# A third group of units in seven forms in one of three gate and up stages of a two-layer trunk

## The chip, the cores and the metric

The kernel runs on one core of a Trainium2 chip. The metric is the device time of one launch in microseconds. The kernel before takes 996.65 us, the median of three runs (996.29 to 997.11).

## The reference, cut to what matters

The trunk has two layers over 256 tokens of width 1024. Each layer is a feed-forward block, a token mixer and a second feed-forward block:

```python
def swiglu(h, w_gate_up, w_down):
    a, b = jnp.split(h @ w_gate_up, 2, axis=-1)
    return (jax.nn.silu(a) * b) @ w_down
...
    x = x + 0.5 * swiglu(rms_norm(x, ffn1_norm), ffn1_w_gate_up, ffn1_w_down)
    h = rms_norm(x, mix_norm)
...
    x = x + merged @ w_out
    x = x + 0.5 * swiglu(rms_norm(x, ffn2_norm), ffn2_w_gate_up, ffn2_w_down)
```

`w_gate_up` is 1024 x 5632 and `w_down` 2816 x 1024, all in float32. The mixer (causal pooling and attention in 256-position blocks, merged by gates) is not touched.

## The kernel before, in words

**Units.** All weights come from DRAM in units of 128 x 2048 float32 (1 MB). A gate and up stage has 22 of them (NF), each with 128 columns of the gate and 128 of the up projection; a down stage has 11. A unit lands in a tile `raw` (four buffers) and is split into `hi` and `lo`, two half tiles each (six half tiles of each kind, so three units): ScalarE copies to float32r (`hi`), VectorE subtracts (`lo`). x is held split in the same way (`hx`). A product of two split operands is then hi by hi and hi by lo' in one 512-wide matmul, and lo by hi in a 256-wide one; a whole unit is 32 matmuls (`pair`), drained from PSUM by one copy and one addition (`drain`).

**Seven forms.** In three of the four gate and up stages, groups of four units are computed in a Strassen scheme. The group's 2 x 2 blocks of weights are combined into seven forms "1" to "7", each of 1 MB and each worth 16 matmuls, so seven half units of work in place of eight. Forms 1, 2 and 3 are blocks of the weights as they are; forms 7, 6, 5 and 4 are sums that POOL's DMAs have written to DRAM before (tiles `f4` to `f7`; `far_sums` lists eight steps for each group, and each call of `go_on` sends one, behind the last marked VectorE instruction). The other operand is a form of x as well: `x_forms` makes four of them (7, 6, 5, 3) on ScalarE and VectorE after unit 2 (XF); forms 1, 2 and 4 use `hx` itself. A group's results have tokens on the partitions and are turned by eight transposes on TensorE (`turned`) before the down stage uses them. Several forms add up in one PSUM bank: 1, 6, 5, 3 in one, 7 and 4 in another, 2 in a third, and between two of them ScalarE or VectorE reads the sum.

**Order.** `feed_order` is a table written out by hand: numbers are whole units, "1A" is form 1 of group A. It is at once the order of the loads on SP's queue, of the splits and of the products on TensorE, which keeps program order. `post` (three VectorE operations, a Silu and a copy) finishes each pair of whole units. Group A is units 12 to 15, group B units 18 to 21.

In the stage that the change is about, the second layer's first gate and up stage (508 to 622 us in the profile), the order before is: 0, 1, 1A, 2, 2A, 3, 4, 7A, 5, 6A, 6, 5A, 7, 4A, 3A, 8, transposes, 1B, 9 with transposes in its middle, 2B, 10, 7B, 11, 6B, 16, 5B, 17, 4B, 3B, and then the down units.

Lines in the profile of before: L99 all matmuls, L549 the transposes, L176 and L177 the two splits of a form (ScalarE, VectorE), L187 and L188 those of a unit, L236 and L237 the drain, L443 to L452 `post`, L497 to L514 `x_forms`, L540 and L541 the gating of a group's results, L566 to L579 what else is done to its banks, L161 POOL's steps.

Of the kernel before, what the change touches and what calls it, by code (L numbers as in the profile page):

```python
# [25 lines left out]
P = 128  # L26
# [17 lines left out]

FU = NF + NF // 2 + 24
LU = FU + NF + NF // 2
GROUPS = {"A": 12, "B": 18}
XF = 2
SHIFT = 16
RAW = {"1": "11", "2": "21", "3": "22"}  # L50
SUMS = (("7", "12", "22"), ("6", "7", "11"), ("5", "11", "12"), ("4", "6", "21"))


def feed_order():

    return [0, 1, "1A", 2, "2A", 3, 4, "7A", 5, "6A", 6, "5A", 7, "4A", "3A", 8, "1B", 9, "2B", 10, "7B", 11, "6B", 16,
            "5B", 17, "4B", "3B"]


def feed_units(base):  # L60
    return [base + n if isinstance(n, int) else (base, n) for n in feed_order()]


C_G1, C_GM, C_G2, C_BG, C_PS, NG = 0, 8, 16, 24, 40, 44
# [3 lines left out]
def trunk_kernel(ctx: ExitStack, tc: tile.TileContext, x_in, w_in, pw_in, qkn_in, rope_in, mask_in, band_in, out):  # L68
# [78 lines left out]
        return z.rearrange("p (i c) -> p i c", i=2)  # L147

    def far_sums(base):
        steps_left.extend((base, g, f, src, kw) for g in GROUPS for f, one, two in SUMS  # L150
                          for src, kw in ((one, {}), (two, {"accum_op": OP.add})))

    def go_on():
# [241 lines left out]
    def bc2(a):  # L395
        return a.unsqueeze(1).to_broadcast([P, 2, a.shape[-1]])

    def ffn(after, n0=0, end=False, col=None, base=0, far_at=()):
        gs, gt = {}, {}

        def room(name, n0, m):
            g = acts.tile([P, m, 2, S], F32R, name=name, tag=name)
            gt[name] = g
            gs.update({n0 + i: g[:, i] for i in range(m)})
# [7 lines left out]
        room("gc", 8, 4)  # L412
        room("gd", 12, 4)
        abs_, more = {}, []
        late_r = not end
        last = {}

        def wide(n):
# [36 lines left out]
        if n0:  # L455
# [6 lines left out]
            for i in range(n0 + 1, NF + 1):  # L462
                if i < NF:
                    pair(unit(), wide(i))
                    fetch()
                    if i >= 8 and i % 3 == 2:
                        go_on()
                if i == NF or i % 3 != 1:
                    for n in range(done, NF if i == NF else min(done + 2, i - 1), 2):
                        scaled = post(n)  # L470
                        done = n + 2
                        if i == n0 + 1:
                            behind(scaled, drained[-1])
        else:
# [6 lines left out]
            columns(ws[1], pss[1], range(4, NK))  # L481
            drain(wide(1), pss[1])

            pre = acts.tile([P, 12 * S], F32, name="pre", tag="gb")
            vt = acts.tile([P, 2, GW], F32, name="vt", tag="v")
            tk = {g: acts.tile([P, 2, GW], F32, name="tk", tag="tok", bufs=2) for g in GROUPS}
            xg = pre[:, :NK * S].rearrange("p (k s) -> p k s", s=S)
            gq = {tn: vt[:, tn // 2, tn % 2 * S:(tn % 2 + 1) * S] for tn in range(4)}
            sf = {}
# [3 lines left out]
            def x_forms():  # L493

                late = drained[-1]
                for k in range(NK):
                    behind(act(xg[:, k, :], x[:, k, :], AF.Copy, scale=gain[:, l_of[0], col + k:col + k + 1]), late)  # L497
                (a11, a21), (a12, a22) = ([z[:, :, t * P:(t + 1) * P] for t in range(2)] for z in (xg[:, :4], xg[:, 4:]))
                s1, s2 = (pre[:, (8 + 2 * i) * S:(10 + 2 * i) * S].rearrange("p (k s) -> p k s", s=P) for i in range(2))
                s3, s4 = (vt[:, i, :].rearrange("p (k s) -> p k s", s=P) for i in range(2))  # L500
                fs = iter(eight(F32R, "sf", SHIFT))

                def parts_of(n, z):
                    sh, sl = (next(fs).rearrange("p (k s) -> p k s", s=P) for _ in range(2))
                    act(sh, z, AF.Copy)
                    tt(sl, z, sh.bitcast(F32), op=OP.subtract)
                    sf[n] = [(sh[:, k, :], sl[:, k, :]) for k in range(4)]

                tt(s3, a11, a21, op=OP.subtract)
                tt(s1, a22, a21, op=OP.subtract)  # L510
                parts_of("7", s3)
                stt(s2, s1, -1.0, a11, op0=OP.mult, op1=OP.subtract)
                parts_of("5", s1)
                stt(s4, s2, -1.0, a12, op0=OP.mult, op1=OP.subtract)  # L514
                parts_of("6", s2)
                parts_of("3", s4)
                room("gb", 16, NF - 16)

            def by_tokens(f, ps, first):

# [22 lines left out]

            def turned(n, g):

                pt = quarter("pt")
                for i in range(2):
                    for t in range(2):
                        keep(nc.tensor.transpose(pt[:, i, t * P:(t + 1) * P], gq[2 * t + n][:, i * P:(i + 1) * P], ident))  # L549
# [5 lines left out]
            bank = {}  # L555

            def strassen(f, g):

                b = ("x" if f in "1653" else "z" if f == "2" else "y") + g
                if b not in bank:  # L560
                    bank[b] = quarter("p" + b).rearrange("p a s -> p (a s)")
                z = bank[b]
                by_tokens(f, z, f in "127")
                p1, w = tk[g][:, 0], tk[g][:, 1]
                if f == "1":
                    act(p1, z, AF.Copy)  # L566
                elif f == "2":
                    tt(p1, z, p1, op=OP.add)
                    gated(p1, 0, 0, 0)
                elif f == "6":  # L570
                    act(w, z, AF.Copy)
                elif f == "5":
                    act(p1, z, AF.Copy)
                    tt(p1, bank["y" + g], p1, op=OP.add)
# [7 lines left out]
            due = None  # L582
            wait = [0, 1]
            for n in feed_order()[2:]:
                if isinstance(n, str):
                    strassen(*n)
                    if n[0] == "3":
                        due = n[1]
                    continue
                if due == "A0":  # L590
                    pair(unit(), wide(n), lambda: turned(0, "A"), NK // 2)
                    due = None
                else:
                    pair(unit(), wide(n))
                fetch()
                if due == "A":
                    turned(1, due)
                    due = "A0"
                if n in (6, 11):
                    go_on()  # L600
                if n == XF:
                    x_forms()
                if n % 2 and n > 1:
                    post(wait[0])
                    wait = [n - 1, n]
            post(wait[0])
            if due:
                last = {(1, 0): lambda: turned(1, due), (1, 5): lambda: turned(0, due)}
# [23 lines left out]
    def add_x(f, ps, two, r):  # L632
        t = x[:, f, :]
        if two:
            t = small.tile([P, S], F32, name="t", tag="sg", bufs=2)
            act(t, ps[:, 1, :], AF.Copy)
            if r is not None:
                tt(t, ps[:, 0, :], t, op=OP.add)
                stt(t, t, 0.5, r, op0=OP.mult, op1=OP.mult)
                marks.append(tt(x[:, f, :], x[:, f, :], t, op=OP.add))  # L640
                return
            stt(t, t, 0.5, x[:, f, :], op0=OP.mult, op1=OP.add)
        stt(x[:, f, :], ps[:, 0, :], 0.5, t, op0=OP.mult, op1=OP.add)

    def tokens():
# [107 lines left out]
    def mix(l, after):  # L753
# [150 lines left out]
        for h in range(NH):  # L904
            gate(h, *((lambda: score_two(h // 2), NK // 2) if h % 4 == 0 else ()))
            if h == 4:
                for p, y in enumerate(ys):
                    heads_end(p, y)
                known = soften_two()
            elif h < 2:  # L910
                soften(h)
            elif h % 4 == 2:
                turn_two(h // 4 * 2, (0, 1) if h > 4 else ())
            elif h == 3:
                pool_diff()
            open_gate(h)
            if h >= 3:
                go_on()

        def branch(f, j, k0=0, k1=4):  # L920
# [87 lines left out]
    for l in range(L):  # L1008
        l_of[0] = l
        if l == 0:  # L1010
            for base in STAGES:
                far_sums(base)
        ffn(lambda f: prep(f, l, C_GM), len(w3) if l == 0 else 0, col=C_G1, base=l * LU, far_at=(1, 3, 5, 7, 9))
        if l == 0:
            for d, z in ((rope, rope_in), (mask, mask_in), (qkn, qkn_in)):
                nc.sync.dma_start(d, z)
        mix(l, lambda f: prep(f, l, C_G2))
        if l + 1 < L:
            ffn(lambda f: prep(f, l + 1, C_G1), col=C_G2, base=FU, far_at=(1, 3, 5, 7, 9))
# [92 lines left out]
```

## Time and profile before

| | |
|---|---|
| profiled execution, own time | 996.52 us |
| its span, first to last instruction | 994.7 us |
| granted TensorE clock | 1.000 |
| busy share of the span: PE, VectorE (DVE), ScalarE (ACT), POOL | 99%, 81%, 65%, 6% |
| the stage from 508 to 622 us: PE, DVE, ACT busy | 114.0, 101.4, 86.8 us |
| DMA in that stage | 273 GB/s, 0.81 of 16 engines busy |

The profile comes from one execution, so a sum over its rows is to be set against 996.52 us. PE is TensorE's matmuls and PEld its weight loads; both overlap. In the rows of the chain of work the columns are start, duration, engine, tile, line and count. In rows of a timeline they are start, duration, engine, line, operation, out<-in, shapes and count, with the idle time before and what ended it in brackets.

### The profile page before, as it was taken

To read this page: it belongs to the slowest core of one execution; us is meant where nothing else is said; L and a number is where in the kernel's file an instruction comes from. 1 tells how busy PE (TensorE), PEld (TensorE's weight loads), DVE (VectorE), ACT (ScalarE), POOL (GpSimd) and SP (SyncE) were. 2 spreads that over 40 slices of the span, in tenths; PEclk is the share of its full clock that TensorE was granted. 3 is DMA by queue.
4 is the path that set the end of the run, shared out by engine and by line. 5 is a ranking of instruction groups with operands and counts; after the bars stand their busy time and mean duration, and the time that the engine had idled before them with its cause. 6 is when DMAs were issued, how large, how long until landed. Compare 5 with 4: busy or idle time off the path is not lost.

```text
span 994.7 us, 16119 instructions
## 1 busy us (share of the span) xinstructions
PE 989.5 (99%) x6312; PEld 898.6 (90%) x6312; DVE 801.1 (81%) x1136; ACT 651.4 (65%) x974; POOL 55.8 (6%) x95
## 2 busy tenths in 40 slices
PE   9999999999999999999999999999999999999998
PEld 8998888898899988889988889888989998888897
DVE  6987777698978799886779888676988888988862
ACT  7865555567756787675578677555677568776641
POOL 0000001002100100000000000000021000000000
PEclk9999999999999999999999999999999999999999
DMA  8878899964889999798966979897858895787740
GB/s 298 319 259 284 249 306 294 293 195 182 275 249 308 351 286 335 251 336 261 300 240 244 299 270 308 304 282 265 261 184 251 268 296 207 260 291 254 254 148 22
DMA packets 45243, 262.11 MB, mean 263 GB/s; under 512 B 4400, under 2 KB 5680, under 8 KB 22448
## 3 DMA queue, kind: packets, MB, share of 16 engines
q1 hardware_dynamic: 34992, 210.76, 57.9%
q0 software_dynamic: 10176, 50.33, 21.2%
q8 instruction: 49, 0.80, 0.3%
q14 instruction: 26, 0.21, 0.1%
HBM read 260.03 MB, written 51.38 MB: 313 GB/s over the span
## 4 chain that ended last, share of the span: by engine, by line
PE 99%; DMA 0%; ACT 0%; DVE 0%; SPq 0%; issue 0%
PE ps L99 72%; PE pt L99 7%; PE two L99 4%; PE pxB L99 3%; PE pxA L99 3%; PE pyA L99 2%; PE pyB L99 2%; PE pe L99 1%; PE sc L99 1%; PE pzB L99 1%; PE pzA L99 1%; PE pt L549 1%; PE pt L739 1%; PE y L99 1%; DMA raw<-w 0%; PE tp L695 0%
## 5 line engine op out<-in xcount | busy, mean ns | idle before, releaser
L188 DVE TENSOR_TENSOR lo<-raw,hi 128x1024 fp32r<-128x1024 f32 (+2 forms) x319 | 378.2, 1197 | 112.5 <-ACT hi L187 110.8
L187 ACT ACTIVATE hi<-raw 128x1024 fp32r<-128x1024 f32 (+2 forms) x319 | 327.8, 1036 | 198.6 <-PE ps L99 126.0
L99 PE MATMUL ps<-hx,hi 128*128 128x512 f32 x1312 | 443.2, 384 | 0.6 <-ACT hi L187 0.6
L99 PE MATMUL ps<-hx,lo 128*128 128x256 f32 x1312 | 358.7, 273 | 0.0
L99 PEld LDWEIGHTS ps<-hx,hi 128*128 128x128 f32 x1312 | 246.2, 188 | 44.6 <-ACT hi L187 0.8
L99 PEld LDWEIGHTS ps<-hx,lo 128*128 128x128 f32 x1312 | 246.5, 188 | 0.3 <-DVE lo L188 0.3
L177 DVE TENSOR_TENSOR lo<-raw,hi 128x1024 fp32r<-128x1024 f32 x84 | 102.2, 1221 | 23.8 <-ACT hi L176 23.7
L176 ACT ACTIVATE hi<-raw 128x1024 fp32r<-128x1024 f32 x84 | 88.9, 1059 | 46.8 <-PE ps L99 31.5
L99 PE MATMUL ps<-ga,hi 128*128 128x512 f32 (+1 forms) x264 | 87.9, 378 | 0.0
L99 PE MATMUL ps<-ga,lo 128*128 128x256 f32 x256 | 70.0, 273 | 0.0
L161 POOL DMA_DIRECT2D f<-w x36 | 33.3, 937 | 594.9 <-DVE ab L237 288.1
L99 PE MATMUL ps<-gb,hi 128*128 128x512 f32 (+1 forms) x198 | 65.4, 376 | 0.0
L99 PE MATMUL pt<-hi,hx 128*128 128x512 f32 x192 | 65.1, 385 | 0.0
L99 PEld LDWEIGHTS ps<-ga,hi 128*128 128x128 f32 x264 | 49.0, 188 | 8.3
L99 PE MATMUL pt<-lo,hx 128*128 128x256 f32 x192 | 52.6, 274 | 0.0
L99 PE MATMUL ps<-gb,lo 128*128 128x256 f32 x192 | 52.4, 273 | 0.0
L99 PEld LDWEIGHTS ps<-ga,lo 128*128 128x128 f32 x256 | 48.1, 188 | 0.0
L99 PE MATMUL ps<-gc,hi 128*128 128x512 f32 (+1 forms) x132 | 44.3, 376 | 0.0
L99 PE MATMUL ps<-gd,hi 128*128 128x512 f32 (+1 forms) x132 | 44.3, 376 | 0.0
L99 PE MATMUL ps<-mk,hi 128*128 128x256 f32 x256 | 44.1, 275 | 0.0
L237 DVE TENSOR_TENSOR ab<-ps,ab 128x512 f32<-128x512 f32 x62 | 42.4, 684 | 0.0
L99 PEld LDWEIGHTS ps<-gb,hi 128*128 128x128 f32 x198 | 36.7, 188 | 6.2
(251 smaller groups left out, 1585.1 us busy)
## 6 DMA issues: line engine op xcount, KB each, us to landing
raw<-w SPq DMA_DIRECT2D x170, 1024.0 KB, 6.9
f<-w POOLq DMA_DIRECT2D x36, 1024.0 KB, 11.8
raw<-f SPq DMA_DIRECT2D x24, 1024.0 KB, 5.5
raw<-w SPq DMA_DIRECT2D x16, 256.0 KB, 5.3
out_dram<-gx SPq DMA_DIRECT2D x8, 128.0 KB, 2.0
gx<-x SPq DMA_DIRECT2D x3, 256.0 KB, 5.6
qk<-pw SPq DMA_DIRECT2D x2, 256.0 KB, 4.7
gx<-x SPq DMA_DIRECT2D x1, 300.0 KB, 2.8
```

The lines of the kernel that those rows point to most:

```text
L99: return keep(nc.tensor.matmul(*args, **kw))
L161: z = nc.gpsimd.dma_start(two_rows(far[f, g, base]), src, **kw)
L176: act(hv, a, AF.Copy)
L177: tt(lv, a, hv.bitcast(F32), op=OP.subtract)
L187: act(hi, w, AF.Copy)
L188: return tt(lo, w, hi.bitcast(F32), op=OP.subtract)
L237: drained.append(tt(t, ps[:, :, 0, :], t, op=OP.add))
L549: keep(nc.tensor.transpose(pt[:, i, t * P:(t + 1) * P], gq[2 * t + n][:, i * P:(i + 1) * P], ident))
L739: keep(nc.tensor.transpose(pt[:, h, o * P:(o + 1) * P], pr[:, h, c * P:(c + 1) * P], ident))
```

## The change

The table becomes two, and each of the three stages picks one. TWO is the order of before under other names: group C is now units 18 to 21. THREE, for the second layer's first stage alone, has a further group B of units 8 to 11, so that ten whole units and 21 forms make up the stage in place of 14 and 14. Its order is: 0, 1, 1A, 2, 2A, 1B, 3, 4, 7A, 6A, 5, 5A, 6, 4A, 2B, 3A, 7B, 6B, 7, both transposes of A, 5B, 16, 1C, 4B, 3B, 6C, 17 with the first transposes of B in its middle, 7C, the second transposes of B, 5C, 2C, 3C, 4C. The transposes of C stand in the down stage, as those of B did before.

```diff
-GROUPS = {"A": 12, "B": 18}
+GROUPS = {"A": 12, "B": 8, "C": 18}
...
+THREE = (0, 1, "1A", 2, "2A", "1B", 3, 4, "7A", "6A", 5, "5A", 6, "4A", "2B", "3A", "7B", "6B", 7, "t0A", "t1A", "5B",
...
+FEED = {FU: TWO, LU: THREE, LU + FU: TWO}
+
+
+def groups_of(base):
+    return "AC" if FEED[base] is TWO else "ABC"
...
-                    if i >= 8 and i % 3 == 2:
+                    if i >= 8 and i % 2 == 0:
                         go_on()
...
+            three = FEED[base] is THREE
+            tk = {g: acts.tile([P, 2, GW], F32, name="tk", tag="tok", bufs=2) for g in ("AB" if three else "AC")}
+            tk.setdefault("C", tk["A"])
+            banks4 = [quarter(f"b{i}").rearrange("p a s -> p (a s)") for i in range(4)]
+            for g in groups_of(base):
+                for f in "1653":
+                    bank[f + g] = banks4[0 if (g == "B" if three else g == "A") else 2]
+                bank["2" + g] = banks4[1]
+                bank["7" + g] = banks4[3]
+                bank["4" + g] = banks4[3]
...
-                pt = quarter("pt")
+                if g == "C":
+                    pt = quarter("pt")
+                else:
+                    pt = (bank["1" + g] if n == three else banks4[1]).rearrange("p (a s) -> p a s", s=S)
...
+            def seven(f, g):
+
+                z = bank[f + g]
+                p1, w = tk[g][:, 0], tk[g][:, 1]
+                if f == "5":
+                    if g == "B":
+                        gated(p1, 0, 0, 0)
+                    if three and g == "C":
+                        p1 = tk["B"][:, 0]
                 by_tokens(f, z, f in "127")
...
                 elif f == "2":
                     tt(p1, z, p1, op=OP.add)
-                    gated(p1, 0, 0, 0)
+                    if g != "B":
+                        gated(p1, 0, 0, 0)
...
-            for n in feed_order()[2:]:
+            xf = iter(())
+            for n in FEED[base][2:]:
+                next(xf, None)
...
-                if n in (6, 11):
+                if n in steps_at:
                     go_on()
                 if n == XF:
-                    x_forms()
+                    xf = x_forms()
+                    for _ in xf if not three else "":
+                        pass
...
-            if h >= 3:
+            for _ in range(2 if h < 3 else 1):
                 go_on()
```

The four banks `b0` to `b3` serve all groups of a stage, where each group had three of its own names before. `x_forms` is now a generator that stops after each of its four parts; in the stage with THREE it goes on by one part at each step of the table, in the others it runs through at once, and its parts stand in the order 7, 6, 5, 3 (7, 5, 6, 3 before). POOL's steps are 56 in place of 48. They are sent after units 8, 10 and so on to 20 of the first stage (8, 11, 14, 17 and 20 before), two after each of the mixer's first three gates (none before), and in the changed stage after units 3, 4, 6 and 16 (6 and 11 before). A new branch of `add_x` is not reached with these tables.

How the rows move, at two places. First VectorE, in the second layer's first stage, at the forms of x. `vt` and `pre` are the sums that the forms are made of, `sf` their low parts, `lo` with four dimensions a form's split and with two a unit's. Before (L514 and L506 are `x_forms`, L177 a form's split):

```order
L514 SCALAR_TENSOR_TENSOR vt<-pre 128x512
L506 TENSOR_TENSOR sf<-pre,sf 128x512
L541 SCALAR_TENSOR_TENSOR vt<-tk,sg 128x256
L237 TENSOR_TENSOR ab<-ps,ab 128x512
L506 TENSOR_TENSOR sf<-vt,sf 128x512
L177 TENSOR_TENSOR lo<-raw,hi 128x2x2x256
L188 TENSOR_TENSOR lo<-raw,hi 128x1024 x2
```

Now (L539 and L527 are `x_forms`, L188 a form's split, L199 a unit's, L248 a drain, L463 the end of a `post`):

```order
L539 SCALAR_TENSOR_TENSOR vt_5314<-pre_5313 128x512
L199 TENSOR_TENSOR lo_5518<-raw_5514,hi_5516 128x1024
L527 TENSOR_TENSOR sf_5412<-pre_5313,sf_5412 128x512
L463 TENSOR_TENSOR ga_5192<-ab_5265,ga_5192 128x2x256
L527 TENSOR_TENSOR sf_5412<-vt_5314,sf_5412 128x512
L188 TENSOR_TENSOR lo_5573<-raw_5570,hi_5571 128x2x2x256
L248 TENSOR_TENSOR ab_5358<-ps_5479,ab_5358 128x512
L188 TENSOR_TENSOR lo_5574<-raw_5570,hi_5572 128x2x2x256
L188 TENSOR_TENSOR lo_5601<-raw_5598,hi_5599 128x2x2x256
L188 TENSOR_TENSOR lo_5602<-raw_5598,hi_5600 128x2x2x256
L199 TENSOR_TENSOR lo_5627<-raw_5624,hi_5625 128x1024
```

Both halves of 7A (lo_5573 and lo_5574) now stand behind the forms of x, where only the second did, and the two halves of 6A follow at once, where unit 5 did.

Second POOL's queue, around the same stage. `f4` to `f7` are the sums in DRAM; the tile's number tells the group. Before:

```order
L161 DMA f5_4883<-w 256x1x1024 x2
L161 DMA f4_5087<-f6_4667 16x16384
L161 DMA f4_5087<-w 256x1x1024
L161 DMA f7_6120<-w 256x1x1024
L769 MEMSET uT_7111 128x4x16
```

Now:

```order
L172 DMA f6_4675<-w 256x1x1024
L172 DMA f5_4891<-w 256x1x1024 x2
L172 DMA f4_5095<-f6_4675 16x16384
L172 DMA f4_5095<-w 256x1x1024
L172 DMA f7_5580<-w 256x1x1024 x2
L797 MEMSET uT_7138 128x4x16
```

The tiles f4_5087 and f4_5095 stand at the same place, but f4_5087 is group B's of the stage itself before, and f4_5095 group C's now, eight steps later in the whole list; behind it both halves of the next stage's f7 are sent ahead of the mixer's memset, where one was.

More of the change, by code (lines that the diff above doesn't have):

```diff
@@ L51 @@
 SUMS = (("7", "12", "22"), ("6", "7", "11"), ("5", "11", "12"), ("4", "6", "21"))
-def feed_order():
-    return [0, 1, "1A", 2, "2A", 3, 4, "7A", 5, "6A", 6, "5A", 7, "4A", "3A", 8, "1B", 9, "2B", 10, "7B", 11, "6B", 16,
-            "5B", 17, "4B", "3B"]
-def feed_units(base):
-    return [base + n if isinstance(n, int) else (base, n) for n in feed_order()]
+TWO = (0, 1, "1A", 2, "2A", 3, 4, "7A", 5, "6A", 6, "5A", 7, "4A", "3A", 8, "t1A", "1C", (9, "t0A"), "2C", 10, "7C", 11, "6C",
+       16, "5C", 17, "4C", "3C")
+THREE = (0, 1, "1A", 2, "2A", "1B", 3, 4, "7A", "6A", 5, "5A", 6, "4A", "2B", "3A", "7B", "6B", 7, "t0A", "t1A", "5B",
+         16, "1C", "4B", "3B", "6C", (17, "t0B"), "7C", "t1B", "5C", "2C", "3C", "4C")
+FEED = {FU: TWO, LU: THREE, LU + FU: TWO}
+def groups_of(base):
+    return "AC" if FEED[base] is TWO else "ABC"
+def feed_units(base):
+    for n in FEED[base]:
+        n = n[0] if isinstance(n, tuple) else n
+        if isinstance(n, int):
+            yield base + n
+        elif n[0] != "t":
+            yield base, n
 C_G1, C_GM, C_G2, C_BG, C_PS, NG = 0, 8, 16, 24, 40, 44
@@ L149, in far_sums @@
     def far_sums(base):
-        steps_left.extend((base, g, f, src, kw) for g in GROUPS for f, one, two in SUMS
+        steps_left.extend((base, g, f, src, kw) for g in groups_of(base) for f, one, two in SUMS
                           for src, kw in ((one, {}), (two, {"accum_op": OP.add})))
@@ L396, in bc2, with ffn @@
         return a.unsqueeze(1).to_broadcast([P, 2, a.shape[-1]])
-    def ffn(after, n0=0, end=False, col=None, base=0, far_at=()):
+    def ffn(after, n0=0, end=False, col=None, base=0, far_at=(), steps_at=()):
         gs, gt = {}, {}
@@ L414, in ffn @@
         abs_, more = {}, []
-        late_r = not end
+        late_r = not (end and FEED[base] is TWO)
         last = {}
@@ L482, in ffn @@
             drain(wide(1), pss[1])
+            bank = {}
             pre = acts.tile([P, 12 * S], F32, name="pre", tag="gb")
             vt = acts.tile([P, 2, GW], F32, name="vt", tag="v")
-            tk = {g: acts.tile([P, 2, GW], F32, name="tk", tag="tok", bufs=2) for g in GROUPS}
+            three = FEED[base] is THREE
[8 more added lines that the diff above has]
+                bank["4" + g] = banks4[3]
             xg = pre[:, :NK * S].rearrange("p (k s) -> p k s", s=S)
@@ L509, in x_forms @@
                 tt(s3, a11, a21, op=OP.subtract)
+                parts_of("7", s3)
+                yield
                 tt(s1, a22, a21, op=OP.subtract)
-                parts_of("7", s3)
                 stt(s2, s1, -1.0, a11, op0=OP.mult, op1=OP.subtract)
+                parts_of("6", s2)
+                yield
                 parts_of("5", s1)
+                yield
                 stt(s4, s2, -1.0, a12, op0=OP.mult, op1=OP.subtract)
-                parts_of("6", s2)
                 parts_of("3", s4)
                 room("gb", 16, NF - 16)
+                yield
             def by_tokens(f, ps, first):
@@ L553, in turned @@
                 tt(g[:, :, 1, :], pt, g[:, :, 0, :].bitcast(F32), op=OP.subtract)
[L555 to L562, printed above, removed]
+            def seven(f, g):
[6 more added lines that the diff above has]
+                        p1 = tk["B"][:, 0]
                 by_tokens(f, z, f in "127")
-                p1, w = tk[g][:, 0], tk[g][:, 1]
                 if f == "1":
@@ L573, in strassen @@
                     act(p1, z, AF.Copy)
-                    tt(p1, bank["y" + g], p1, op=OP.add)
+                    tt(p1, bank["7" + g], p1, op=OP.add)
                     gated(p1, 1, 1, 1)
@@ L580, in strassen @@
                     gated(w, 1, 0, 0)
-            due = None
             wait = [0, 1]
-            for n in feed_order()[2:]:
+            xf = iter(())
+            for n in FEED[base][2:]:
+                next(xf, None)
                 if isinstance(n, str):
-                    strassen(*n)
-                    if n[0] == "3":
-                        due = n[1]
+                    (turned if n[0] == "t" else seven)(*((int(n[1]), n[2]) if n[0] == "t" else n))
                     continue
[L590 to L594, printed above, removed]
+                n, t = n if isinstance(n, tuple) else (n, None)
+                pair(unit(), wide(n), *([lambda: turned(int(t[1]), t[2]), NK // 2] if t else ()))
                 fetch()
-                if due == "A":
-                    turned(1, due)
-                    due = "A0"
-                if n in (6, 11):
+                if n in steps_at:
                     go_on()
                 if n == XF:
-                    x_forms()
+                    xf = x_forms()
+                    for _ in xf if not three else "":
+                        pass
                 if n % 2 and n > 1:
@@ L606, in ffn @@
             post(wait[0])
-            if due:
-                last = {(1, 0): lambda: turned(1, due), (1, 5): lambda: turned(0, due)}
+            last = {(1, 0): lambda: turned(1, "C"), (1, 5): lambda: turned(0, "C")}
         order = [divmod(b, NF) for b in (
@@ L642, in add_x @@
             stt(t, t, 0.5, x[:, f, :], op0=OP.mult, op1=OP.add)
+        elif r is not None:
+            z = small.tile([P, S], F32, name="t", tag="sg", bufs=2)
+            stt(z, ps[:, 0, :], 0.5, r, op0=OP.mult, op1=OP.mult)
+            tt(t, t, z, op=OP.add)
+            return
         stt(x[:, f, :], ps[:, 0, :], 0.5, t, op0=OP.mult, op1=OP.add)
@@ L1012, in trunk_kernel @@
                 far_sums(base)
-        ffn(lambda f: prep(f, l, C_GM), len(w3) if l == 0 else 0, col=C_G1, base=l * LU, far_at=(1, 3, 5, 7, 9))
+        ffn(lambda f: prep(f, l, C_GM), len(w3) if l == 0 else 0, col=C_G1, base=l * LU, far_at=(1, 3, 5, 7, 9), steps_at=(3, 4, 6, 16))
         if l == 0:
@@ L1018, in trunk_kernel @@
         if l + 1 < L:
-            ffn(lambda f: prep(f, l + 1, C_G1), col=C_G2, base=FU, far_at=(1, 3, 5, 7, 9))
+            ffn(lambda f: prep(f, l + 1, C_G1), col=C_G2, base=FU, far_at=(1, 3, 5, 7, 9), steps_at=(6, 11))
         else:
```

## The prediction

> **What bounds the kernel now.** I read the page first, then what TensorE waited for, then the chain of work, then the stretches of time of the one stage that changes. From the page, the busy time of each engine:
>
> ```profile
> PE 989.5 (99%) x6312; PEld 898.6 (90%) x6312; DVE 801.1 (81%) x1136; ACT 651.4 (65%) x974; POOL 55.8 (6%) x95
> ```
>
> PE is busy for 989.5 us, 99% of the span. What it waited for in the whole execution is two rows:
>
> ```profile
> PE busy L99 <- DVE eps L276: 1.1, 1, 1.1
> PE ps L99 <- ACT hi L187: 0.6, 1, 0.6
> ```
>
> So there is no wait left on PE to remove: 1.7 us in all, both at the start. Time can come only from less PE work, and anything that makes PE wait is paid in full. The chain of work (start, duration) over the second layer's first gate and up stage gives the price of each kind of PE work:
>
> ```profile
> 532.46 2.68 PE pyA L99 x16
> ...
> 556.56 2.72 PE pyA L99 x16
> 559.28 2.71 PE pxA L99 x16
> 561.99 5.36 PE ps L99 x32
> 567.35 0.44 PE pt L549 x4
> 567.79 2.68 PE pxB L99 x16
> 570.47 2.68 PE ps L99 x16
> 573.15 0.44 PE pt L549 x4
> 573.59 2.67 PE ps L99 x16
> 576.25 2.76 PE pzB L99 x16
> 579.01 5.35 PE ps L99 x32
> 584.36 2.68 PE pyB L99 x16
> 587.04 5.35 PE ps L99 x32
> 592.39 2.69 PE pxB L99 x16
> ...
> 600.43 2.68 PE pxB L99 x16
> ...
> 608.46 2.72 PE pyB L99 x16
> 611.18 2.71 PE pxB L99 x16
> ```
>
> Rows `ps` are whole units (32 matmuls), rows `px`, `py`, `pz` one form (16 matmuls), rows `pt` four transposes. There are no gaps between them. The pyA of 532.46 is form 7A, that of 556.56 is 4A.
>
> **PE's own sum.** Units 8, 9, 10 and 11 go: 5.36 + (2.68 + 2.67) + 5.35 + 5.35 = 21.41 us (the rows at 561.99, 570.47 and 573.59, 579.01, 587.04). Seven forms come; those of group B in the rows above, in the order 1, 2, 7, 6, 5, 4, 3, cost 2.68 + 2.76 + 2.68 + 2.69 + 2.68 + 2.72 + 2.71 = 18.92 us. Two sets of four transposes come: 2 x 0.44 = 0.88 us. That is 19.80 us for 21.41, so 1.61 us less. One correction: a form right behind a form took 2.71 (3A and 3B), behind a unit 2.68 or 2.69 (6 and 5). The new order has some ten more such neighbours, so up to 10 x 0.03 = 0.3 us back; I take 0.2. PE's work falls by 1.4 us (1.3 to 1.6).
>
> [...]
>
> **What else changes on PE: the banks of PSUM.** Three groups now share four banks in place of one set per group, so a form can wait for an older value's reader. The tightest place is 5C, 2C, 3C: 3C adds into the bank from which ScalarE must first have copied 5C, so the copy has one form, 2.7 us. On ScalarE the copy stands behind the second split half of 4C, whose buffer PE gives free at the end of 5C. Rows for such a copy and such a split:
>
> ```profile
> 551.43 0.59 ACT L573 ACTIVATE tk<-pxA 128x512 f32<-128x512 f32 x1
> 551.91 1.05 ACT L176 ACTIVATE hi<-raw 128x1024 fp32r<-128x1024 f32 x1
> ```
>
> 1.1 + 0.6 = 1.7 us of 2.7: about 1 us is left, and I cost it at nothing; if ScalarE is late PE waits 1 to 2 us once. The other reuses have at least two PE steps between, except the 2B/3A/7B run, where 7B overwrites the bank of 4A two forms later (5.4 us).
>
> **VectorE.** Stage and rows that price it:
>
> ```profile
> 508.00:622.00 114.00, 114.00 (x687) 102.38 (x688) 101.42 (x126) 86.76 (x117) 2.90 (x4) 1.00 0.81 273
> ```
> ```profile
> 526.80 0.68 DVE L512 SCALAR_TENSOR_TENSOR pre<-pre 128x512 f32<-128x512 f32 x1
> 527.40 0.69 DVE L506 TENSOR_TENSOR sf<-pre,sf 128x512 fp32r<-128x512 f32 x1
> ...
> 530.75 1.22 DVE L177 TENSOR_TENSOR lo<-raw,hi 128x1024 fp32r<-128x1024 f32 x1
> 531.88 2.36 DVE L188 TENSOR_TENSOR lo<-raw,hi 128x1024 fp32r<-128x1024 f32 x2
> ...
> 549.61 1.23 DVE L177 TENSOR_TENSOR lo<-raw,hi 128x1024 fp32r<-128x1024 f32 x1 [0.85 <-ACT hi L176]
> ```
>
> The columns of the stretch are PE, PEld, DVE, ACT and POOL busy, granted clock, DMA share and GB/s. One split takes 1.14 us of VectorE in a queue (531.88 less 530.75), a 512-wide operation 0.60 (527.40 less 526.80). The change adds three units' worth of splits, 6 x 1.14 = 6.8; takes four drains and two times three operations of `post`, 10 x 0.60 = 6.0; adds a group's ends, five 512-wide operations (3.0) and four narrow ones (some 1.2, at half the price). So VectorE goes from 101.4 to some 106.4 us of a stage that is 112.6 us long: 94%, no bound by itself, but near enough that its order matters. Two places:
>
> At the forms of x, 7A's second split ended at 530.75 + 1.22 = 531.97, and PE came to it half a form after 532.46, at 533.80: 1.8 us of lead, the smallest in the stage. In the new order 1B stands ahead: two splits, 2.28 us, on VectorE, 2.69 us on PE; the lead becomes 2.2. 6A now follows 7A at once: done at 534.25 + 2.28 = 536.5, wanted at 537.83 + 1.34 = 539.2: 2.6 us.
>
> In the run 4A, 2B, 3A, 7B, 6B the lead at 4A is 557.92 less 550.84, 7.1 us. From there to the middle of 6B PE takes 4 x 2.69 = 10.8 us; VectorE has 8 splits (9.1), seven 512-wide operations (4.2) and two narrow ones (at most 0.7 together by half the 512-wide price): 14.0. The lead falls to some 3.9 us and is not used up. Both at no cost; without the cover PE would wait what VectorE is late.
>
> **Transfers.** Here are the stretches and, for 508 to 622, the queues and landings:
>
> ```profile
> 182.00:334.00 152.00, 152.00 (x1094) 140.96 (x1092) 125.00 (x209) 98.44 (x172) 17.72 (x23) 1.00 0.80 259
> 556.00:564.00 8.00, 8.00 (x49) 7.15 (x48) 6.89 (x9) 6.36 (x8) 0.00 (x0) 1.00 1.01 224
> 564.00:572.00 8.00, 8.00 (x52) 7.21 (x51) 5.22 (x7) 4.44 (x7) 0.00 (x0) 1.00 0.97 398
> ```
> ```profile
> q1 hardware_dynamic: 4341, 27.96, 67.9%
> q0 software_dynamic: 793, 3.09, 12.8%
> ...
> raw<-w SPq DMA_DIRECT2D x21, 1024.0 KB, 6.8
> ```
>
> A load (1.05 MB) costs 0.679 x 114 / 26.7 = 2.9 us of all engines, a step of POOL 0.128 x 114 / 2.95 = 5.0 us. Eight steps are added. Two fall into the first stage (10 us more of transfers), six into the first layer's mixing (0.80 x 152 + 30 = 151.6 of 152: full). PE takes a unit in 5.3 us there and a load of 1 MB needs 2.9, so loads keep up beside steps that take the rest; POOL's steps may slip into the next stage. I cost both at nothing, with up to 1 us if a slipped step meets the next stage's first forms. In the changed stage three more forms in all means three more loads. The full stretch is some 528 to 564: eight loads (5A, 6, 4A, 2B, 3A, 7B, 6B, 7) and three steps (at units 3, 4 and 6), 8 x 2.9 + 3 x 5.0 = 38 us for 36. The loads have slack: that for unit 6 is issued when 7A's split frees its buffer (534.3) and PE comes to 6 at 548.5; less 1.05 + 1.22 us of splitting and 6.8 of landing, 5.1 us is left. 2 us late is hidden.
>
> **Sum.** The profiled execution took 996.52 us; less 1.4 is 995.1. The median of the three runs, 996.65, lies 0.13 above it, so 995.2 is my number. A difference of 0.2%, 2.0 us, is about what a measurement of this kernel can tell from no change; the forecast, 0.14% down, lies inside it.
>
> **The rivals.** *Small waits* (same, chance 0.18): VectorE late at 7A or 6A, or ScalarE at 3C, or a slipped step. For: leads of 1.0, 2.2 and 2.6 us worked out from one execution. Against: 1.8 us at 7A was enough before. Price 0.5 to 3 us: 995.7 to 998.2.
>
> *Transfers bound the run 4A to 7* (slower, 0.08): 11 transfers of 1.05 MB, 11.5 MB, in 36 + 5 us need 280 GB/s. The stretch 556 to 564 moved 224 GB/s at a full share, 564 to 572 398. At 398 all is landed in 29 us; at 224 it takes 51 us, and PE stops for 10 us: 1005. It is slower by over 0.2% from a stop of 3.5 us on, below 258 GB/s. Against it: the stretch 508 to 622 landed its loads in 6.8 us in the median with a step in flight. [...]
>
> *Transposes at the pace of the matmuls* (faster, 0.08): 16 matmuls of 384 columns in the mean take 2.67 us, so 128 columns 0.056 us and eight transposes 0.44 in place of 0.88, above all as two sets now stand in a row (5.36 us of unit, then eight). Then 21.41 - 18.92 - 0.44 = 2.05 us: 994.5. Every row of four at 0.44 speaks against it.
>
> **How the numbers follow.** The forecast, PE without a gap, has 0.66; with the small waits 0.84 is within 0.2% (994.7 to 998.6), 0.08 slower, 0.08 faster. The range goes from 994.5 (the third rival) to 997.4, which takes in two thirds of the small waits and leaves out the transfers' stop and the worst of the waits.
>
> **What would show it.** Right: PE's waits still about 1.7 us; 6304 matmuls and transposes for 6312; the piece from 7A to the first down unit, 532.46 to 611.18 + 2.71 = 613.89 and so 81.4 us long before, at 81.4 - 1.4 - 2.7 (1B now stands ahead of it) = 77.3 us; PE rows of forms at 2.67 to 2.76 and of transposes at 0.44. Wrong: a wait of PE on a split near 7A, 6A or 6B with VectorE busy throughout (VectorE); with ScalarE waiting for a load (transfers); on ScalarE's copy at 3C (banks); or a stage shorter by 2 us or more (transposes).

## The result, and the profile after

The changed kernel takes 1006.17 us in the median of six runs (1000.67 to 1007.6) beside 996.78 for the kernel before (996.29 to 998.67): a ratio of 1.008, with a 95% interval from 1.0064 to 1.0096. It is slower by 0.8%, where 995.2 us, "within 0.2%", was forecast and 997.4 was the upper end of the range.

The profiled execution took 1001.66 us (span 999.9, granted clock 1.000); it is the second fastest of the six. Its busy times, and what TensorE waited for in the whole execution (in total, times, the longest):

```profile
PE 989.7 (99%) x6304; PEld 896.8 (90%) x6304; DVE 804.9 (80%) x1141; ACT 653.9 (65%) x981; POOL 62.5 (6%) x103
```
```profile
PE b L110 <- DVE tk L603: 2.2, 1, 2.2
PE b L577 <- DVE vt L566: 1.2, 1, 1.2
PE busy L110 <- DVE eps L287: 1.1, 1, 1.1
PE b L110 <- ACT tk L600: 0.7, 2, 0.4
PE b L110 <- ACT tk L602: 0.5, 1, 0.5
PE ps L110 <- ACT hi L198: 0.5, 1, 0.5
```

The two waits at the start (eps and the first hi) were there before. The other rows are new; with two of 0.3 us that are not shown they make 5.2 us, of the 6.5 between 995.2 and 1001.66. Note where they lie: the wait of 1.2 us (line 577, the transposes of group A) is at 394 us, in the first layer's second gate and up stage, whose order of units and forms the change leaves as it was; the one of 2.2 us is at 558 us, at form 4A of the changed stage.

The stretches of both stages, first before, then after (columns as in the prediction; POOL's count in brackets is mostly its DMA steps there):

```profile
334.00:393.00 59.00, 59.00 (x354) 52.93 (x354) 54.88 (x73) 47.82 (x66) 1.72 (x2) 1.00 0.95 318
...
509.00:568.00 59.00, 59.00 (x354) 52.93 (x354) 52.81 (x70) 45.91 (x64) 1.03 (x1) 1.00 0.77 256
```
```profile
334.00:393.00 59.00, 59.00 (x352) 52.72 (x351) 50.50 (x68) 45.01 (x63) 5.58 (x7) 1.00 1.00 328
393.00:449.00 56.00, 54.80 (x332) 49.21 (x332) 50.17 (x59) 40.47 (x54) 1.54 (x2) 1.00 0.98 350
...
509.00:568.00 59.00, 56.44 (x334) 49.93 (x334) 51.86 (x68) 48.05 (x67) 2.74 (x3) 1.00 0.79 272
```

Between 334 and 393 us POOL sends seven steps where it sent two, and the DMA engines are full (1.00). Six of the seven were written ahead of this stage and had not been started by 334 us: 26 of the 32 steps written ahead had, where it was 23 of 24 before. POOL's steps started one behind another, and two of the rows below, those with "DMA" in brackets, stood for 19 and 20 us until an earlier step had landed.

```profile
324.66 1.03 POOL L172 DMA_DIRECT2D f<-w  x1 [19.07 <-DMA f<-w]
339.49 0.53 POOL L172 DMA_DIRECT2D f<-f  x1 [13.80 <-DVE a L332]
348.06 1.75 POOL L172 DMA_DIRECT2D f<-w  x2 [8.04 <-DVE ab L248]
369.98 1.03 POOL L172 DMA_DIRECT2D f<-w  x1 [20.18 <-DMA f<-w]
...
```

The loads then land later. Median time from issue to landing between 334 and 449 us, before and after:

```profile
raw<-w SPq DMA_DIRECT2D x21, 1024.0 KB, 7.4
```
```profile
raw<-w SPq DMA_DIRECT2D x21, 1024.0 KB, 9.8
```

How such a load reaches TensorE is seen at 4A of the changed stage. The chain of waits (start, duration):

```profile
540.63 13.12 DMA raw<-w
553.86 1.07 ACT hi L187
...
557.23 0.68 DVE tk L603
```

and ScalarE's timeline over the same time:

```profile
551.77 0.57 ACT L247 ACTIVATE ab<-ps 128x512 f32<-128x512 f32 x1
553.86 2.00 ACT L187 ACTIVATE hi<-raw 128x1024 fp32r<-128x1024 f32 x2 [1.51 <-DMA raw<-w]
555.77 0.58 ACT L602 ACTIVATE tk<-b 128x512 f32<-128x512 f32 x1
```

2B's load took 13.1 us. Its split stands in ScalarE's queue ahead of the copy of 5A's bank (line 602), so that the copy, the addition on VectorE (line 603) and 4A, which overwrites that bank, wait for a load that 4A has no use for. The stop at 394 us hangs on a late load as well: the chain that leads to it has one of 13.43 us from 374.77 on. Is that order the cause, or only the place at which late loads are felt? And is the dense stage to blame, or the eight added steps?

### The profile page after: what moved, and what is told of

The parts are those of the page before. It is cut to its first block, busy times and chain, and to the rows that moved or that the text cites. A ratio compares the mean times of both kernels' runs of the same rounds, so it can differ in the third digit from the quotient of the medians.

```text
span 999.9 us, 16135 instructions
## 1 busy us (share of the span) xinstructions
PE 989.7 (99%) x6304; PEld 896.8 (90%) x6304; DVE 804.9 (80%) x1141; ACT 653.9 (65%) x981; POOL 62.5 (6%) x103
## 4 chain that ended last, share of the span: by engine, by line
PE 84%; DMA 7%; DVE 5%; issue 2%; ACT 2%; SPq 0%; ACTq 0%; DVEq 0%
PE ps L110 62%; PE pt L110 7%; PE b L110 7%; DMA raw<-w 6%; PE two L110 4%; DVE lo L188 2%; PE pe L110 1%; DMA raw<-f 1%; DVE lo L199 1%; PE sc L110 1%; ACT hi L198 1%; PE pt L767 1%; PE y L110 1%; ACT hi L187 1%; DVE ab L248 0%
## 5 line engine op out<-in xcount | busy, mean ns | idle before, releaser
L199 DVE TENSOR_TENSOR lo<-raw,hi 128x1024 fp32r<-128x1024 f32 (+2 forms) x311 | 367.9, 1195 | 114.1 <-ACT hi L198 110.3
L110 PE MATMUL ps<-hx,hi 128*128 128x512 f32 x1248 | 421.7, 384 | 0.5 <-ACT hi L198 0.5
L110 PE MATMUL ps<-hx,lo 128*128 128x256 f32 x1248 | 341.3, 273 | 0.0
L110 PEld LDWEIGHTS ps<-hx,hi 128*128 128x128 f32 x1248 | 234.2, 188 | 42.5 <-ACT hi L198 0.7
L110 PEld LDWEIGHTS ps<-hx,lo 128*128 128x128 f32 x1248 | 234.5, 188 | 0.4 <-DVE lo L199 0.3
L188 DVE TENSOR_TENSOR lo<-raw,hi 128x1024 fp32r<-128x1024 f32 x98 | 118.3, 1218 | 20.1 <-ACT hi L187 19.9
L187 ACT ACTIVATE hi<-raw 128x1024 fp32r<-128x1024 f32 x98 | 102.1, 1054 | 40.6 <-PE ps L110 16.0
L110 PE MATMUL b<-hi,sf 128*128 128x512 f32 x224 | 77.1, 385 | 1.2 <-ACT tk L600 0.7
L110 PE MATMUL b<-lo,sf 128*128 128x256 f32 x224 | 61.5, 274 | 0.0
L110 PE MATMUL b<-hi,hx 128*128 128x512 f32 x168 | 51.9, 389 | 2.2 <-DVE tk L603 2.2
L110 PEld LDWEIGHTS b<-hi,sf 128*128 128x128 f32 x224 | 42.0, 188 | 9.6 <-ACT tk L600 1.2
```

What stands on the lines that cost most here:

```text
L110: return keep(nc.tensor.matmul(*args, **kw))
L187: act(hv, a, AF.Copy)
L188: tt(lv, a, hv.bitcast(F32), op=OP.subtract)
L199: return tt(lo, w, hi.bitcast(F32), op=OP.subtract)
```

## The experiments

All ratios are to the kernel before, run on the same chip in turn.

**again**: the changed kernel, as it is.

> The changed kernel once more, for a second trace: the first came from an execution of 1001.66 us, where the median is 1006.17. The transfers' theory (POOL's steps fill the DMA engines in the changed stage and the one before it, loads land after 9 to 13 us, and results that PE waits for stand behind their splits) expects 1001 to 1008 us, PE's stops in the same places, longer, each with ScalarE waiting for a load just before. The VectorE theory (the denser forms alone are too much for VectorE) expects the same time, with VectorE busy without idle time before each stop.

Measured: 1003.7 us (1002.42 to 1009.58), a ratio of 1.0081 (95% interval 1.005 to 1.0112). The stops of the same code differ from one execution to the next: 1.4 and 0.6 us in the first layer's stage here, 0.8 and 2.3 in the changed one. And the clock shows something new. The stop of 2.3 us ended at 559.88; these are stretches of two microseconds from there on:

```profile
558.00:560.00 2.00, 0.12 (x1) 0.12 (x2) 2.00 (x4) 1.45 (x3) 0.00 (x0) 1.00 1.01 428
560.00:562.00 2.00, 2.00 (x10) 1.74 (x11) 2.00 (x4) 1.91 (x4) 0.00 (x0) 0.82 1.01 426
562.00:564.00 2.00, 2.00 (x9) 1.71 (x8) 2.00 (x3) 2.00 (x5) 0.00 (x0) 0.50 0.90 377
564.00:566.00 2.00, 2.00 (x11) 1.76 (x11) 2.00 (x4) 1.24 (x2) 1.03 (x1) 0.83 0.66 184
```

By what is missing to 1.00 in each stretch, the granted clock is halved for (0.18 + 0.5 + 0.17) x 2 / 0.5 = 3.4 us. That costs 1.7 us more if matmuls then take twice as long, an estimate. The nearest measured pace is that of early_lu (below) at 0.50: four matmuls of a form in 1.28 us (starts at 561.30 and 562.58), for 0.68 at 1.00 (80 in 13.50 us in no_sums).

**no_sums**: POOL's steps are left out. Forms 4 to 7 load a block of the weights in place of their sums, so the loads and the work of the engines stay, and the result is not the reference.

```diff
-        src = quadrant(base, g, RAW[f]) if f in RAW else two_rows(far.pop((f, g, base)))
+        src = quadrant(base, g, RAW.get(f, "12"))
...
-            for base in STAGES:
-                far_sums(base)
```

> All 56 steps of POOL are taken away, and forms 4 to 7 load one block of the weights where they loaded a sum; so the sums are left out, and the work of PE, ScalarE and VectorE and the bytes of the loads stay. The transfers' theory expects PE's stops gone: the time that was forecast, 994.8 to 996 us, and loads landing in 5 to 6 us in the stage. The VectorE theory expects no difference: 1000 us or more, with 4 us or more of stops in the changed stage.

Measured: 995.35, 0.9985 (0.9975 to 0.9994). TensorE waits only at the start, with VectorE as busy in the stage as in any kernel here (56.24 of the 59 us from 509 to 568). That refutes the theory that the denser forms are too much for VectorE. The chain from 7A to the first down unit has no gap:

```profile
535.55 5.36 PE b L110 x32
...
554.29 13.50 PE b L110 x80
...
573.15 0.87 PE b L577 x8
...
612.61 5.35 PE ps L110 x32
```
```profile
PE busy L110 <- DVE eps L287: 1.1, 1, 1.1
PE ps L110 <- ACT hi L198: 0.8, 1, 0.8
```

So TensorE's work and VectorE's load are what the prediction said; what was lost came with POOL's steps.

**steps_late**: in the changed stage one step in place of four (the list is then done later).

```diff
-far_at=(1, 3, 5, 7, 9), steps_at=(3, 4, 6, 16))
+far_at=(1, 3, 5, 7, 9), steps_at=(16,))
```

> The changed kernel with one step of POOL in the changed stage, after unit 16, in place of four after units 3, 4, 6 and 16; the other three move to the down stage and the mixer behind it. The transfers' theory expects the loads of 6 to 7B to land in 5 to 7 us where they took 9 to 13, the stop of 2.2 us at 4A gone, the 1.2 us in the stage before it unchanged, and 2 to 6 us less than the changed kernel: 998 to 1003. The VectorE theory expects no difference of over 1 us.

Measured: 1003.21, 1.0078 (1.0043 to 1.0112). The changed stage has no stop over 0.4 us; the first layer's has one of 2.9 us at its own 4A, and with it 3.4 us at half clock (0.85, 0.50 and 0.80 in the stretches of two microseconds from 384 us on). So the stop in the changed stage came with the steps sent there early, and the one in the first layer's stage with other steps.

**fetch_last**: the next form's load and split are written behind a form's result operations.

```diff
-                fetch()
...
+                fetch()
```

> The changed kernel with the next load and split written behind a form's result operations, where they stood ahead of them. The order theory (it is the place in the in-order queues that turns a late load into a stop: 5A's copy and addition stand behind the split of 2B, which waits for its load) expects loads as late as before, but the stop at 4A gone and 1 to 3 us less: 999 to 1005. If lateness of the splits themselves is what counts, it expects no gain, or up to 3 us more, since each split starts later: 1002 to 1010.

Measured: 1006.36, 1.0097 (1.0082 to 1.0112). This tells little: in the order that ran, ScalarE still had the split of 2B ahead of the copy of 5A, and the stops stayed (1.7 and 2.1 us at 4A of the two stages).

**three_48**: the changed stage's order as it is, but the third group's sums are left out; its forms 4 to 7 load a block of the weights, so the result is not the reference. POOL's 48 other steps go where the kernel before sends them (after unit 16 in place of 11 in the changed stage). The diff is cut:

```diff
-        steps_left.extend((base, g, f, src, kw) for g in groups_of(base) for f, one, two in SUMS
+        steps_left.extend((base, g, f, src, kw) for g in "AC" for f, one, two in SUMS
...
```

> The changed kernel with the third group's eight sums left out, and POOL's 48 other steps sent where the kernel before sends them (after units 8, 11, 14, 17, 20 of the first stage, none after the mixer's first three gates, after units 6 and 16 of the changed stage). The forms 7, 6, 5 and 4 of the third group load a block of the weights in place of their sums, so the loads and the work on the engines are those of the change, and what they compute is not the reference. Theory (the eight added steps overfill the DMA engines; the denser stage by itself does no harm): 995.2 to 996.5, no stop of TensorE over 1 us. Rival (the stage's denser loads and splits, with even two steps of POOL beside them, stop TensorE): a stop of 2 us or more at 4A is left, 997.5 to 999.

Measured: 995.36, 0.9988 (0.9977 to 0.9999), no stop beyond the start over 0.2 us. Two steps between 334 and 393 us.

**before_more**: the order before, with eight more steps of POOL, for sums that nothing reads, and all 56 sent at the change's places. The diff is cut:

```diff
+MORE = {"A": 12, "B": 18, "C": 8}
...
+        steps_left.extend((base, g, f, src, kw) for g in (MORE if base == LU else GROUPS) for f, one, two in SUMS
...
```

> The kernel before with eight more sums, of units 8 to 11 of the changed stage, which nothing reads, sent with the changed kernel's places for POOL's steps. Work on TensorE, VectorE and ScalarE and the loads are those of the kernel before. Theory (the eight added steps by themselves): a stop of 1 to 3 us in the stage from 334 to 393 us as POOL's steps slip there, with or without some of it in the second layer's stage: 998 to 1005. Rival (the steps do harm only beside the denser stage's loads): 996.5 to 997.2, TensorE's waits at 1.7 us.

Measured: 1004.41, 1.007 (1.0053 to 1.0087). The waits of TensorE and the first layer's stretch:

```profile
PE pyA L100 <- DVE tk L575: 2.0, 1, 2.0
PE pxA L100 <- ACT tk L572: 1.5, 1, 1.5
```
```profile
334.00:393.00 59.00, 56.99 (x333) 50.78 (x332) 50.73 (x66) 43.67 (x61) 5.59 (x7) 0.97 1.00 328
```

These two runs separate the two halves of the change. The dense stage alone costs nothing. The eight steps alone, at the change's places, cost 7.4 us (1004.41 beside 996.97 for the kernel before), which is most of the loss. Here the other stage has a stop of 1.5 us too, with two groups in it: the steps need no dense stage to do harm.

**three_last** and **last_spread**: the third group moved to the last gate and up stage. In three_last the eight added steps are sent in the second mixing; last_spread sends four of the list's steps more ahead of the first layer's second stage, and none more in the second mixing. The diff, cut to what both share:

```diff
-FEED = {FU: TWO, LU: THREE, LU + FU: TWO}
+FEED = {FU: TWO, LU: TWO, LU + FU: THREE}
...
```

> The table with the third group moved to the second layer's last gate and up stage; POOL's steps in the first stage, the first layer's mixing and the changed stage are where the kernel before has them, the eight added ones go into the second layer's mixing (two after each of its first three gates). Theory (the added steps harm where they slip into a stage of forms or fill a stretch): 995.2 to 996 if the second mixing takes them, 997 to 1003 with a stop of 1 to 3 us at the start of the last stage if they slip there. Rival (three groups in a stage are too dense whatever the steps): a stop of 2 us or more at 4A of the last stage, 997 or more.

> As the kernel with the third group in the last gate and up stage, but with the eight added steps spread: two more in the first stage (after units 8, 10, 12 and so on), two after the first layer's first two gates, the second mixing as before, and the rest of the list shifts. Theory: no stop over 1 us, 994.9 to 995.8, 0.1 to 0.2% under the kernel before. Rival (three groups in a stage are too dense): 997 or more with a stop at 4A of the last stage. Rival (two more steps in the first mixing slip into the stage behind it already): a stop of 1 to 3 us between 334 and 393 us, 996.5 to 1000.

Measured: three_last 995.67, 0.9989 (0.9978 to 0.9999); last_spread 995.38, 0.9983 (0.9974 to 0.9992). Neither has a new wait on TensorE, and last_spread beats both kernels, by 0.17% of the one before. Its first layer's stage bears three steps with the engines at 0.96:

```profile
334.00:393.00 59.00, 59.00 (x355) 52.97 (x354) 54.87 (x72) 48.00 (x67) 2.24 (x3) 1.00 0.96 316
```

In three_last the added steps slip as well, but not as far. These are its second mixing up to 818 us and, behind it, the beginning of the last gate and up stage (its first unit starts at 825.98, its first form at 828.76):

```profile
760.00:818.00 58.00, 58.00 (x493) 56.73 (x492) 48.57 (x81) 36.73 (x60) 5.59 (x7) 1.00 0.96 293
818.00:880.00 62.00, 62.00 (x373) 55.56 (x373) 55.77 (x74) 50.78 (x72) 2.59 (x3) 1.00 0.98 341
```

Seven steps run in the mixing, where TensorE waits for nothing, and three in the stage of forms with its three groups, which bears them without a stop.

**swap_2b**: 2B ahead of 4A in the table.

```diff
-6, "4A", "2B", "3A"
+6, "2B", "4A", "3A"
```

> The changed kernel with 2B and 4A changing places in the table of the changed stage (5A, 6, 2B, 4A, 3A). All of POOL's steps stay. The result of 5A has then one form more, 2.7 us, before 4A needs it, and 2B itself is wanted 2.7 us earlier. Theory (4A stops because the copy of 5A's bank stands on ScalarE behind 2B's split, which waits for a late load): the stop at 4A goes or falls under 0.6 us, and TensorE waits for 2B's split instead, 0.5 to 1.5 us; 1000 to 1005 in all, since the first layer's stops stay. Rival (the result of 5A is late for a cause of its own on VectorE): the wait at 4A stays near 2 us.

Measured: 1006.25, 1.0102 (1.0084 to 1.012), above the range that was expected. The wait at 4A of the changed stage went, as the theory has it, but TensorE did not wait for 2B's split: a stop of 2.3 us came at 7B, which overwrites 4A's bank. The first layer's stage, which is that of the change again, stopped for 3.6 us.

**early_lu** and **fu_more**: the third group where the change puts it, four steps taken out of the first mixing. early_lu has five in the changed stage; fu_more has three more in the down half of the first layer's second stage and two in the changed one. The first edit is in both, the second in fu_more alone:

```diff
-            for _ in range(2 if h < 3 else 1):
+            if h != 2:
                 go_on()
...
-col=C_G2, base=FU, far_at=(1, 3, 5, 7, 9)
+col=C_G2, base=FU, far_at=(1, 2, 3, 5, 6, 7, 9, 10)
```

> The changed kernel with four of the added steps taken out of the first mixing's gates (two after the first two gates stay) and POOL's steps in the changed stage after units 3, 4, 6, 7 and 16. Theory: the first layer's second stage has no stop over 0.5 us, since fewer steps slip into it (3 in place of 7 between 334 and 393 us); the stop of about 2 us at 4A of the changed stage stays: 997 to 1000. Rival (the full transfers of the mixing are not what stops it): a stop of 1 us or more between 334 and 400 us stays.

> As the last, but three of the steps go into the down half of the first layer's second stage (three more of its 11 units send one) and the changed stage has two (after units 6 and 16). The third group is where the change puts it. Theory (only where the steps stand costs): no stop over 0.6 us, 995.0 to 996.0, under the kernel before by 0.1 to 0.2%. Rival (the denser stage cannot bear steps at all once sums are really read, or the down half is filled in turn): a stop of 1 us or more in or ahead of the changed stage, 996.5 to 999.

Measured: early_lu 1007.4, 1.0107 (1.0092 to 1.0122); fu_more 997.93, 1.0009 (0.9995 to 1.0023). In both the stops of the first layer's stage are gone, with three steps in it in place of seven. But early_lu, expected at 997 to 1000, is no faster than the change: it stops at 4A of the changed stage for 4.8 us, with the first two steps at the same places as in the change. Both have another stop at 3C, of 3.0 and 2.2 us, which has a cause of its own. SP's queue and ScalarE's in fu_more:

```profile
SPq L182 <- DMA f<-w: 7.3, 1, 7.3
```
```profile
607.82 2.00 ACT L187 ACTIVATE hi<-raw 128x1024 fp32r<-128x1024 f32 x2 [1.25 <-DMA raw<-f]
609.73 0.58 ACT L602 ACTIVATE tk<-b 128x512 f32<-128x512 f32 x1
```

4C's load waited 7.3 us for its own sum, whose last step had been sent only at 586.2 and landed after 13.5 us; the copy of 5C's bank stood behind its split. In early_lu SP waited 8.4 us in the same way.

In the changed stage the count of steps alone does not decide, then. Seven profiles have two steps there, those after units 3 and 4, that started 5 to 6 us apart between 533 and 545 us: the change, again, fetch_last, before_more, swap_2b, early_lu and copy_first. Each of them has a stop of 1.3 to 4.8 us between 550 and 575 us. Of the eight without that pair, only sum_early (below) has one there, of 1.0 us.

**copy_first**: after every form 5, the split fetched next is held behind the copy and the addition.

```diff
+        first = hold.pop() if hold else None
...
+            if first:
+                behind(one, first[0])
+                behind(two, first[1])
...
+                    hold.append((act(p1, z, AF.Copy), tt(p1, bank["7" + g], p1, op=OP.add)))
...
```

> The changed kernel, POOL's steps and tables as they are, but in every group the copy of form 5's bank on ScalarE and the addition behind it on VectorE are held ahead of the split of the form three places later, whose load may be late. Theory (the stops come from results that stand in the queues behind a split that waits for a load): TensorE's waits on tk at 4A, in both stages, and at 3C fall from 2 us and more to under 0.6 us each; what is left is the late split itself, 0 to 1.5 us at the form behind 4A: 996.5 to 1001 in all. Rival (the late loads stop TensorE whatever the order of the queues): the stops of 2 us and more only move one form on, to a wait on a split, and the time stays at 1003 to 1007.

Measured: 1007.36, 1.0109 (1.0074 to 1.0144). TensorE's largest waits:

```profile
PE b L110 <- DVE lo L190: 2.6, 3, 1.3
PE b L583 <- DVE vt L572: 2.1, 1, 2.1
PE b L110 <- ACT hi L190: 1.9, 2, 1.6
```

The waits at 4A and 3C are gone, and nothing is gained: TensorE now waits for the splits themselves, 0.3 to 1.6 us at a time, and again for the transposes (2.1). In the first layer's stage, where these splits waited for loads, 3.8 us are lost, no less than the 1.2 to 3.6 in the other profiles. That speaks for the rival: there the order decided where a late load was felt, and not what it cost. For the whole kernel this run is no clean test, since the new order makes a stop of its own: on ScalarE 2C's split began only at 612.99, right behind the copy of 5C's bank at 612.49 and with no wait for a load, and TensorE stood for 1.6 and 0.5 us. The clock fell there as well: 0.98 from 568 to 618 us and 0.99 from 618 to 760, after 1.00 in every stretch from 30 to 568.

**sum_early**: fu_more with its last two steps after units 3 and 6 in place of 6 and 16.

```diff
-steps_at=(6, 16))
+steps_at=(3, 6))
```

> The kernel with the three steps moved into the down half of the first layer's second stage, with the last two steps of the list after units 3 and 6 of the changed stage in place of 6 and 16. Theory (the stop of 2.2 us at 3C came from 4C's own sum, which landed 7.3 us after its load could have started): SP's queue has no wait on a sum, the stop at 3C goes, no stop over 0.6 us: 994.9 to 996.0, 0.1 to 0.2% under the kernel before. Rival (the stage's transfers are full with any two steps among its loads): a stop of 1 us or more at 4A or 3C stays, 996.5 to 1000.

Measured: 996.66, 0.9999 (0.999 to 1.0009). SP waits for no sum, and the stop at 3C is gone, as the theory of the late sum has it. A stop of 1.0 us is left in the changed stage, at the form behind the transposes of A, where a copy stands behind a split that waits for a load. So the third group can stay in its place, with all 56 steps, without a loss, but not with a gain that is measured.

## Why the prediction was wrong, point by point

*PE's own sum* was right: without POOL's steps the kernel takes 995.35, for 995.2 forecast, and 7A to the first down unit takes 612.61 - 535.55 = 77.1 us, for 77.3. Forms in a row take 2.70 (13.50 for five), eight transposes 0.87; the third rival (transposes at the matmuls' pace) is refuted by that row.

*VectorE* was right: at 56.24 of 59 us busy it made TensorE wait nowhere in no_sums.

*PSUM's banks*: right in the place and in the order on ScalarE (5C's copy behind 4C's split, "1 to 2 us once" if late), and it happened: 0.5 us in the change, 2.2 and 3.0 in two variants. What made the copy late was not foreseen: the load of the split ahead of it.

*Transfers* is the step that failed: "loads keep up beside steps that take the rest; POOL's steps may slip into the next stage. I cost both at nothing, with up to 1 us". The slip came about as described, and its price was wrong: it was set by a mean over the 152 us of the mixing, where the steps did not get done. Seven steps in 59 us filled the engines of the next stage, and the median landing went from 7.4 to 9.8 us, with single loads over 13. That stage lost 1.2 to 3.8 us in the seven profiles that had seven steps there, with nothing lost in the eight that had three or fewer. In the changed stage "2 us late is hidden" failed in the same way: the slack of 5.1 us at a landing of 6.8 us (worked out for unit 6) is gone at 11.9, and 2B's load took 13.1. The sum of transfers, 38 us for 36, was no better guide: over 509 to 568 us the share was 0.79, hardly above the 0.77 before. The prediction's own sign for this step, a wait of TensorE with ScalarE waiting for a load, is what the traces show.

*The rivals*: the one on the other side, "transfers bound the run 4A to 7", had the cause and one of the two places, at a chance of 0.08, too little. It was priced by bandwidth over the run, a stop of 10 us or none; what came was a late load here and there, 1 to 5 us each. That its 1005 us lie near the measured time is luck: no single stop of 10 us came, and part of the loss lies in another stage.

*The clock.* Every stretch in the prediction stands at a granted clock of 1.00; these runs show it halved. All four stops of 2.9 us or more came with a drop. That of steps_late (2.9) brought 3.4 us and the longest of early_lu (4.8) 6.8 us (0.88, three times 0.50 and 0.92 in the stretches of two microseconds from 556 us on), both from within the stop on. For the stops of 3.6 in swap_2b and 3.0 in early_lu there are stretches of ten microseconds, at 0.83 and at 0.95 and 0.88; if the drop is to 0.50 there too, each is 3.4 us long. From 2.0 to 2.3 us it goes either way: a stop of 2.3 (again) brought 3.4 us at half clock, and those of 2.0 (before_more) and 2.1 (fetch_last) a stretch of ten microseconds at 0.83, as much by the same sum, while those of 2.2 in the change's own profile and in fu_more, 2.3 in swap_2b and 2.1 in copy_first did not (1.00 in the stretches around them). What decides it there, no run shows.

How 1002 to 1007 come together: in swap_2b's profiled execution (1005.28) the waits that are not at the start are 3.6 + 2.3 + 1.6 = 7.5 us, and one drop of the clock 1.7: 995.3 + 9.2 = 1004.5. The change's own median of 1006.17 belongs to executions that have no profile, so its sum can't be made in the same way. Their mean clocks are on record, though: the two executions at 1.000 took 1000.67 and 1001.66 us, the four at 0.997 to 0.999 took 1005.95 to 1007.6. A drop of 3.4 us takes 0.002 off the mean (again's profiled execution, with one, stands at 0.998), so by an estimate from that most of the slower four had one drop or two, at 1.7 us each. That does not make up a difference of 4 us and more, so they must also have had longer stops than the profile shows; where those lie is not known.

What stays open: how much of the cost of late loads another order of the queues could hide, since copy_first adds a stop of its own; and why the same code stops for 1.2 us in one execution and 3.6 in another.

## What to carry to other kernels

Work that is moved to a background queue is priced in the stage where it really runs: follow the queue past the stage it was written in, and look at the landing of single loads there, not at a mean share. Here the late loads set the time, and three tries at another order (fetch_last, swap_2b, copy_first) gained nothing; sending the steps elsewhere did. Cost an added piece of background work by itself, with the dense work left out, and the other way round: three_48 and before_more told most of the story here.

## What the runs showed of the hardware

Of eleven stops of TensorE of 2.0 us or more, seven came with a drop of its granted clock: to 0.50 for 3.4 us in again (a stop of 2.3) and steps_late (2.9), and for 6.8 us with the longest, 4.8 in early_lu. In again the drop began 1.4 us after the work had resumed, as the 0.82 of that stretch gives. A wait of 2 us with such a drop costs up to 3.7, by the estimate of 1.7 us for a drop. And the first layer's second stage, with the same instructions and the same steps of POOL in all four, stopped for 1.2 us in the change's profile, 2.0 in again, 2.9 in steps_late and 3.6 in swap_2b: with the engines at 1.00, a single profile says little about the size of a loss.
